# A kernel's first stage: small loads first, tokens and modulation weights in turn, tensor work in the order of landing, dummy products in the waits

## The chip, the cores and the metric

One core of a Trainium2 chip. The metric is the time of one execution on the device in microseconds; the median over several runs counts. A profiled execution gives the rows shown here.

## The reference

One layer of a hybrid backbone on 128 context tokens and 512 latent tokens of width 1024, all in float32. Each half has its own conditioning vector (`c_ctx` or `c`):

```python
mod = jax.nn.silu(cond) @ w_mod + b_mod
shift, scale, gate = jnp.split(mod, 3, axis=-1)
h = _rms(x, norm_pre_w) * (1 + scale[:, None, :]) + shift[:, None, :]
u = h @ w_in          # z, xbc, dt, q, k, v, g
...
out = mix @ w_out
y = x + gate[:, None, :] * _rms(out, norm_post_w)
```

Between `u` and `mix` stand a Mamba-2 scan (16 heads) and a retention scan (8 heads), both in two directions, in chunks of 128 tokens. The outputs are `y` for both halves and the context's final scan states.

## The kernel before

The 640 tokens are five token tiles t of 128 (tile 0 is the context), the model width is eight row blocks k of 128. A float32 product is made of three products of a faster type: each operand is split in a rounded part (`hh`, `w0h`, `whi`) and the rest (`hl`, `w0l`, `wlo`), and high x high, high x low and low x high are summed in PSUM.

The kernel has three parts: the first stage, which is in question; then a long middle in which the columns of `w_in` stream through 116 weight pieces (`ws`) while the scans are run as small jobs between the products; then the output product. The first stage makes the modulated tokens `h` (split, transposed, `hh` and `hl`), which the whole middle reads, and beside it multiplies them with the first 512 columns of `w_in` into five PSUM banks (`acc`, one a token tile). When the last of these is done, the first products of the middle (`gt`) follow.

The order of the first stage is written out by hand in `START`, a text of operations that a loop near line 352 emits. A letter is an operation, the number behind it is k or t:

- `M` (`load_wm`, L247): loads modulation weights of block k, 1024 KB, on SP's queue; three buffers. `W` (`load_w0`, L252): loads the block of `w_in`, 256 KB; three buffers. `L` (`load_x`, L258): loads a token tile, 512 KB; five buffers. `C`: two tables of 520 and 256 KB that the middle needs.
- `N` (`norm_x`): the token tile's sum of squares on ACT (L274), its power -0.5 on POOL, and the scaling of its first 128 columns on DVE (L279). `R` (`rest_x`): scales the other 896.
- `A` (`mod_a`): 16 TensorE records that multiply silu of the conditioning with the modulation block (`mod<-wm,silc`), and a copy `ms` on DVE (L297). `B` (`mod_b`): four products that turn the result into columns (`mod<-idt,ms`), and two DVE operations that make shift and scale of the block (`ash`, L317 and L318).
- `S` (`split0`): `w0h` on ACT (L306) and `w0l` on DVE.
- `H` (`h_tile`): for block k and the listed token tiles, transposes on TensorE (`tr`, L325), shift and scale on ACT (L329), and the split into `hh` (L332) and `hl` on DVE. It needs `B` of the block and `N` (or `R`) of the tokens.
- `G` (`gemm0`): three products `acc` of 512 columns for each listed token tile. It needs `H` and `S`.
- `Z` (`warm`): four dummy products of 128 x 128 zeros (`warm<-wz`) for each unit of its number; nothing reads them.
- `F` (`feed`): loads the first pieces of the middle's weights.

The transposes, `A` with `B`, and `Z` share three PSUM banks (`pi`); `A`'s bank is held until both `ash` are made. Each engine works its instructions in order. The order of the text is a preference: the framework that builds the kernel plans each engine's queue from it, and can put an instruction whose operands come earlier ahead of one that stands before it. The packed constants `pk` (108 KB: conditioning vectors, norms, biases) and `idt` (65 KB: the identity for the transposes) are loaded on ACT's queue at the start (lines 141 and 142).

Of the kernel before, what the change touches and what calls it, by code (L numbers as in the profile page):

```python
# [25 lines left out]
Z0, XS0, B0, C0, DT0, Q0, K0, V0, G0 = 0, 1024, 2048, 2560, 3072, 3104, 3616, 4128, 5152  # L26
# [15 lines left out]


START = """
M0 Z2 W0 L0 L1 L2 L3 L4 M1 W1 M2 N0 S0 A0 B0 H0:0 G0:0 R0 Z4 N1 H0:1 N2 N3 R1 H0:2 G0:1 H0:3 W2 M3
N4 W4 R2 R3 H0:4 R4 A1 S2 G0:4 W3 G0:3 B1 S1 S3 G0:2 H1:4 A2 W5 H1:0123 M4 B2 M5 H2:012 H2:3 H2:4
G1:01 G1:2 G2:12 G2:3 A3 G1:34 G2:4 B3 H3:0123 S4 G2:0 A4 H3:4 M6 G3:012 B4 H4:0123 H4:4 A5 G3:34 C0
M7 W7 S5 W6 B5 H5:0123 G4:012 A6 G4:34 F2 S6 B6 H5:4 H6:0123 H6:4 G5:012 A7 G5:34 F2 B7 S7 H7:0123
G6:34 G6:012 H7:4 F2 G7:012 G7:34
"""  # L50


# [53 lines left out]
def body(ctx, tc, io):  # L106
    nc = tc.nc
    vec, act, pool, sp, pe = nc.vector, nc.scalar, nc.gpsimd, nc.sync, nc.tensor
# [28 lines left out]
    pk = const.tile([P, PK_N], F32, name="pk")  # L137
    cst = const.tile([P, CN], F32, name="cst")
    idt = const.tile([P, P + 2], F32, name="idt")
    rope = const.tile([P, 4, 2, 64], F32, name="rope")  # L140
    act.dma_start(out=pk, in_=io["pk"])
    act.dma_start(out=idt, in_=io["idt"])
    tl = const.tile([P, 1], F32, name="tl")
    vec.memset(tl, 0.0)
    act.activation(tl, tl, AF.Tanh)
# [1006 lines left out]
```

## Time and profile before

| | |
|---|---|
| median of 3 runs | 608.21 us (607.2 to 610.53) |
| profiled execution | 606.02 us, its span 604.0 us, mean granted clock 0.993 |
| TensorE, VectorE, ScalarE, GpSimd busy | 582.3, 418.1, 337.4, 31.3 us |
| moved by DMA | 87.44 MB, 145 GB/s on average |
| first product of the middle | at 62.74 us of the span |

A slice of the page is 15.1 us long, so the first stage is the first four of 40. PE is TensorE's products, PEld its weight loads, DVE is VectorE, ACT is ScalarE, POOL is GpSimd, SP issues nearly all loads. A name such as `acc<-w0h,hh` is the written tile and the read ones. An engine that is 96% busy by this count need not be at its peak, since matrix products are pipelined and their ends are modelled.

### The profile page before, as it was taken

The page shows a single profiled execution, that of the slowest core. Times are in us where ns is not written, and L with a number is a line of the kernel's source. Part 1 is how long each engine was busy: PE and PEld are TensorE (multiplying, and loading weights), DVE is VectorE, ACT ScalarE, POOL GpSimd, SP SyncE. Part 2 cuts the span into 40 slices and gives each one's busy share as a digit, 9 for nine tenths or more (in the row PEclk, how much of TensorE's full clock was granted, in tenths as well). Part 3 has the DMA queues.
Part 4 walks back from the last instruction along what each step waited for, and adds up shares of the span by engine and source line. Part 5 has one row for each costly group of instructions (what it writes and reads, how often), then busy time and mean ns, then how long its engine had stood idle before and what let it go on. Part 6 is the DMA issues. An engine that isn't in the chain of part 4 may idle for free.

```text
span 604.0 us, 10966 instructions
## 1 busy us (share of the span) xinstructions
PE 582.3 (96%) x3833; PEld 521.5 (86%) x3833; DVE 418.1 (69%) x942; ACT 337.4 (56%) x934; POOL 31.3 (5%) x112
## 2 busy tenths in 40 slices
PE   5899998999999999999999999999999999999995
PEld 3577998978999998889999888999999777788895
DVE  3657498855698866668897746798867866743665
ACT  5436255665667764465766646566755857262421
POOL 1000001200000010000011000000110000000010
PEclk9899999999999999999999999999999999999998
DMA  8694231553335633232554223354537777384033
GB/s 348 229 362 161 63 105 48 162 146 109 99 97 159 185 91 86 80 122 70 189 172 112 76 69 105 102 163 131 160 96 223 209 266 221 116 272 120 18 109 135
DMA packets 47638, 87.44 MB, mean 145 GB/s; under 512 B 5792, under 2 KB 18656, under 8 KB 46048
## 3 DMA queue, kind: packets, MB, share of 16 engines
q1 hardware_dynamic: 47296, 86.57, 45.2%
q8 instruction: 30, 0.49, 0.3%
q14 instruction: 24, 0.20, 0.1%
q10 hardware_dynamic: 288, 0.18, 0.1%
HBM read 75.03 MB, written 9.60 MB: 140 GB/s over the span
## 4 chain that ended last, share of the span: by engine, by line
PE 65%; DVE 13%; ACT 9%; DMA 6%; issue 5%; POOL 2%; SPq 0%; POOLq 0%; DVEq 0%; ACTq 0%
PE gw L123 24%; PE gc L123 11%; PE gt L123 9%; PE acc L123 5%; PE go L123 4%; DMA cf<-cumd 3%; PE ss L123 2%; PE mod L123 2%; DVE wlo L131 2%; DVE SC L128 2%; PE sfb L123 1%; PE ry L123 1%; POOL sm L131 1%; DVE yc L128 1%; ACT jk L733 1%
## 5 line engine op out<-in xcount | busy, mean ns | idle before, releaser
L131 DVE TENSOR_TENSOR wlo<-raw,whi 128x512 fp32r<-128x512 f32 (+1 forms) x120 | 82.2, 690 | 49.2 <-ACT whi L174 48.3
L174 ACT CAST whi<-raw 128x512 fp32r<-128x512 f32 (+1 forms) x120 | 73.6, 619 | 76.3 <-PE gw L123 46.1
L123 PE MATMUL gc<-hh,whi 128*128 128x320 f32 x384 | 96.7, 331 | 0.0
L123 PE MATMUL gc<-hl,whi 128*128 128x320 f32 x384 | 88.3, 310 | 0.0
L123 PE MATMUL gc<-hh,wlo 128*128 128x320 f32 x384 | 87.6, 309 | 0.0
L123 PEld LDWEIGHTS gc<-hh,whi 128*128 128x128 f32 x384 | 63.9, 189 | 1.1
L123 PEld LDWEIGHTS gc<-hl,whi 128*128 128x128 f32 x384 | 64.3, 188 | 0.1
L123 PEld LDWEIGHTS gc<-hh,wlo 128*128 128x128 f32 x384 | 64.1, 188 | 0.0
L123 PE MATMUL gw<-whi,hh 128*128 128x512 f32 x120 | 50.6, 421 | 0.8 <-ACT u L484 0.8
L123 PE MATMUL gw<-whi,hl 128*128 128x512 f32 x120 | 47.0, 392 | 0.0
L123 PE MATMUL gw<-wlo,hh 128*128 128x512 f32 x120 | 46.8, 390 | 0.0
L123 PE MATMUL gt<-whi,hh 128*128 128x256 f32 (+1 forms) x160 | 46.3, 289 | 0.0
L123 PE MATMUL gt<-wlo,hh 128*128 128x256 f32 (+1 forms) x160 | 45.7, 286 | 0.0
L123 PE MATMUL gt<-whi,hl 128*128 128x256 f32 (+1 forms) x160 | 45.7, 286 | 0.0
L862 ACT ACTIVATE m<-gu,dt 128x128 f32<-128x128 f32 x80 | 31.3, 391 | 16.5 <-DVE gu L131 14.6
L834 ACT ACTIVATE cf<-cf,dmc 128x128 f32<-128x128 f32 x80 | 26.5, 393 | 18.4 <-DMA cf<-cumd 18.4
L131 DVE TENSOR_TENSOR m<-m,cf 128x512 f32<-128x512 f32 x40 | 27.5, 689 | 8.8 <-ACT cf L863 8.2
L123 PE MATMUL gw<-whi,mrh 128*128 128x512 f32 x80 | 32.3, 404 | 0.0
L123 PE MATMUL gw<-wlo,mrh 128*128 128x512 f32 x80 | 31.2, 391 | 0.0
L123 PEld LDWEIGHTS gt<-whi,hh 128*128 128x128 f32 x160 | 30.5, 190 | 0.7 <-issue 0.5
L863 ACT ACTIVATE cf<-gu,dt 128x128 f32<-128x128 f32 x80 | 31.0, 387 | 0.0
L123 PE MATMUL gw<-whi,mrl 128*128 128x512 f32 x80 | 30.9, 391 | 0.0
(232 smaller groups left out, 1327.8 us busy)
## 6 DMA issues: line engine op xcount, KB each, us to landing
raw<-ws SPq DMA_DIRECT2D x116, 256.0 KB, 2.8
cf<-cumd SPq DMA_DIRECT2D x20, 512.0 KB, 4.2
wm<-wm SPq DMA_DIRECT2D x8, 1024.0 KB, 8.2
mraw<-mixd SPq DMA_DIRECT2D x16, 320.0 KB, 3.4
ef<-ecumd SPq DMA_DIRECT2D x32, 128.0 KB, 3.3
wg<-wg SPq DMA_DIRECT2D x4, 1024.0 KB, 5.9
x<-x SPq DMA_DIRECT2D x5, 512.0 KB, 7.3
mixd<-rmix SPq DMA_DIRECT2D x20, 128.0 KB, 2.7
```

The lines of the kernel that those rows point to most:

```text
L123: r = pe.matmul(out, lhsT=a, rhs=b, start=start, stop=stop)
L128: eng.scalar_tensor_tensor(out=out, in0=in0, scalar=s, in1=in1, op0=op0, op1=op1)
L131: return eng.tensor_tensor(out=out, in0=a, in1=b, op=op)
L174: act.copy(hi, raw)
L733: act.activation(jk, yc[:, h], AF.Square, scale=P ** -0.5, accum_out=sm[:, 2 + h:3 + h])
L834: act.activation(cf[:, e, 1, q], cf[:, e, 1, q], AF.Identity, bias=dmc[:, c, h:h + 1])
L862: act.activation(m[:, e, q], gu[:, 0], AF.Copy, scale=dt[:, c, h:h + 1])
L863: act.activation(cf[:, e, 1, q], gu[:, 1], AF.Copy, scale=dt[:, c, 16 + h:17 + h])
```

## The change

`pk` and `idt` go to SP's queue, ahead of all other loads. The order of the first stage is rewritten:

- Loads: before, M0, W0, all five tokens, M1, W1, M2. After: L0, M0, W0, L1, L2, M1, W1, L3, L4, M2.
- Dummies: before, Z2 at the start and Z4 behind the first token's products (24 products). After: Z14 at the start, then Z1, Z4, Z3 and Z2 (96 products).
- Work: block 1 for tokens 0 to 2 (`H1:012`, `G1:012`) comes ahead of tokens 3 and 4. From block 3 on, `B` and `H` of the next block stand behind both halves of `G`, where they stood between the halves or further ahead.
- The second stage's first pieces (first `F2`) are loaded ahead of W6, M7 and W7, where they stood behind them.

```diff
-M0 Z2 W0 L0 L1 L2 L3 L4 M1 W1 M2 N0 S0 A0 B0 H0:0 G0:0 R0 Z4 N1 H0:1 N2 N3 R1 H0:2 G0:1 H0:3 W2 M3
-N4 W4 R2 R3 H0:4 R4 A1 S2 G0:4 W3 G0:3 B1 S1 S3 G0:2 H1:4 A2 W5 H1:0123 M4 B2 M5 H2:012 H2:3 H2:4
-G1:01 G1:2 G2:12 G2:3 A3 G1:34 G2:4 B3 H3:0123 S4 G2:0 A4 H3:4 M6 G3:012 B4 H4:0123 H4:4 A5 G3:34 C0
-M7 W7 S5 W6 B5 H5:0123 G4:012 A6 G4:34 F2 S6 B6 H5:4 H6:0123 H6:4 G5:012 A7 G5:34 F2 B7 S7 H7:0123
-G6:34 G6:012 H7:4 F2 G7:012 G7:34
+L0 M0 W0 L1 L2 M1 W1 L3 L4 M2 Z14 N0 S0 A0 Z1 B0 H0:0 Z4 N1 G0:0 R0 H0:1 Z3 N2 R1 G0:1 H0:2 A1 S1 R2 G0:2 B1
+H1:012 N3 W2 Z2 G1:012 H0:3 M3 N4 G0:3 R3 A2 H0:4 H1:3 G0:4 R4 G1:3 B2 H1:4 S2 G1:4 H2:0123 H2:4 W3 M4
+G2:012 A3 G2:34 B3 S3 H3:0123 W4 H3:4 M5 G3:012 A4 G3:34 B4 S4 H4:0123 H4:4 W5 C0 M6 G4:012 A5 G4:34 F2
+B5 S5 H5:0123 H5:4 W6 M7 G5:012 A6 G5:34 F2 B6 S6 H6:0123 H6:4 W7 G6:012 A7 G6:34 F2 B7 S7 H7:0123 H7:4
+G7:012 G7:34
...
-    act.dma_start(out=pk, in_=io["pk"])
-    act.dma_start(out=idt, in_=io["idt"])
+    sp.dma_start(out=pk, in_=io["pk"])
+    sp.dma_start(out=idt, in_=io["idt"])
```

## The prediction

> **What bounds the kernel now.** I read the page first, then the chain of waits in order of time for the first 80 us, then the windows and the timeline of the same stretch.
>
> ```profile
> span 604.0 us, 10966 instructions
> ...
> PE   5899998999999999999999999999999999999995
> ```
>
> TensorE is the bound, except in the first two of 40 slices (15.1 us each). Whatever the change can win lies there; behind it time is only shifted. The span of 604.0 belongs to an execution of 606.0 us, 2.2 under the median of 608.2; I predict a difference and put it on the median.
>
> ```profile
> 6.88 1.98 PE mod L123 x16
> ...
> 20.13 1.87 PE mod L123 x16
> ...
> 35.10 0.34 PE mod L123 x4
> ...
> 52.21 1.00 PE mod L123 x16
> 53.21 1.60 PE acc L123 x6
> 54.81 0.34 PE mod L123 x4
> 55.15 0.50 PE tr L325 x4
> 55.65 3.49 PE acc L123 x15
> 59.14 0.11 PE tr L325
> 59.24 3.49 PE acc L123 x15
> 62.74 15.99 PE gt L123 x120
> ```
>
> Columns: start, duration, who. The first stage ends at 62.74, where the second one's products (gt) begin. Warm prices: the 15 products of one row block k (G) 3.49, its 16 modulation products (A) 1.00, its 4 selecting products (B) 0.34, a transpose 0.11 to 0.13. One block is 3.49 + 1.00 + 0.34 + 5 x 0.12 = 5.4, eight are 43.5 us. So 19 us of the stage are no work. The page hides one cause:
>
> ```profile
> 10.00:12.00 2.00, 1.31 (x10) 1.16 (x11) 0.89 (x4) 1.04 (x4) 0.54 (x1) 1.00 1.02 420
> ...
> 16.00:18.00 2.00, 0.55 (x3) 0.26 (x2) 1.49 (x6) 0.84 (x3) 0.83 (x1) 1.00 0.97 404
> 18.00:20.00 2.00, 1.14 (x3) 0.45 (x2) 1.80 (x5) 0.46 (x1) 0.00 (x0) 0.76 1.10 439
> 20.00:22.00 2.00, 2.00 (x18) 0.67 (x17) 0.00 (x0) 0.00 (x0) 0.00 (x0) 0.50 0.86 346
> ```
>
> Columns: stretch, then busy time of PE, PEld, DVE, ACT, POOL, then granted clock, DMA share, GB/s. PE waits from 16 to 19 for the last token tiles, and then real work runs at clock 0.50: the same 16 modulation products cost 1.87 at 20.13 and 1.00 at 52.21. All loads together run at 404 to 439 GB/s until 22.
>
> **The change, part by part.** *Loads.* These rows are the issue of the third modulation block M2, its landing, and the loads issued between 1 and 2 us (size, us from issue to landing):
>
> ```profile
> 7.44 0.43 SPq L247 DMA_DIRECT2D wm<-wm  x1
> ```
> ```profile
> wm<-wm SPq DMA_DIRECT2D x1, 1024.0 KB, 11.4
> ```
> ```profile
> x<-x SPq DMA_DIRECT2D x1, 512.0 KB, 6.5
> raw<-w SPq DMA_DIRECT2D x1, 256.0 KB, 5.7
> pk<-pk ACTq DMA_DIRECT2D x1, 108.0 KB, 5.4
> idt<-idt ACTq DMA_DIRECT2D x1, 65.0 KB, 5.9
> ```
>
> M2 lands at 7.44 + 11.4 = 18.84. Before M2 the two orders load the same set (pk, idt, M0, M1, W0, W1, five tokens), so M2 lands there again, and the others lie ahead of it by their sizes at 420 GB/s, 410 KB per us: L4 16.3, L3 15.1, W1 13.8, M1 13.2, L2 10.7, L1 9.5, W0 8.2, M0 7.6. The gain is M1. Its place in the old order is behind all tokens: M1 then lands one M2 and one W1 ahead of 18.84, 15.7, and PE reached it at 20.13. The loss is that the first modulation products start near 7.6 and not 6.88.
>
> *The move of pk and idt.* On ACT's queue their issues took 0.41 and 0.46; on SP's they stand ahead of all loads:
>
> ```profile
> 0.72 0.41 ACTq L141 DMA_DIRECT2D pk<-pk  x1
> 1.16 0.46 ACTq L142 DMA_DIRECT2D idt<-idt  x1
> ```
> ```profile
> SPq L258 <- DMA pk<-pk: 2.3, 1, 2.3
> ```
>
> The first token's issue starts 0.9 later than M0's did, at 1.6. The engines stay idle until about 2 anyway, so every landing slips by 0 to 0.9; I take 0.3, since 173 small KB are under way meanwhile. pk, which landed at 0.72 + 5.4 = 6.1 and held the first products, lands near 3 and is off the path; should it stay late, M0 at 7.6 covers it. ACT is freed 0.9 earlier, which nobody waits for. The last row shows SP's ninth load waiting for the landing of the first one (pk). In the new order these partners (L0 ahead of L4, M0 ahead of M2) land long before the engines run dry: 0. In a sentence of its own: the Trainium skill, "DMA: Bandwidth & Descriptors", section "Issuing engines are not separate DMA queues", says that loads issued by different engines share the same 16 engines and that a second issuer saves issue time only. The trace agrees (pk, 108 KB, took 5.4 us from its own queue beside M0); by that rule alone the move costs its 0.9 of issue and the result would be 0.6 above mine.
>
> *Dummy products.*
>
> ```profile
> 11.33 1.91 PE L123 MATMUL warm<-wz 128*128 128x128 bf16 x16
> ```
>
> Cold, they start every 0.107 us: Z14 is 56, ends at 1.0 + 6.0 = 7.0 at the latest and delays nothing that lands at 7.6. Z1, Z4, Z3, Z2 (40 products, at most 4.3 cold, half of that warm) stand in the waits for tokens 1, 2 and M1; PE is in order, so one that comes late holds real products for at most 1.9: I take 0, range 0 to 1.
>
> In sentences of their own: the Trainium skill, "TensorE: Matmul & The Clock Gate", part 1, says that the array runs at half rate by default, at full rate after a busy window of 3.4 us, and falls back after an idle one. The trace agrees in the fall (clock 0.50 after the wait of 16 to 19); by the rule PE would be at full rate from 7 on.
>
> *PE's work up to B3.* With M1 at 13.2 + 0.3, A1 ends at 14.5. What follows is priced by this chain for the fourth block:
>
> ```profile
> 35.70 0.22 DVE L317 TENSOR_SCALAR ash<-mod,pk 128x2 f32<-128x2 f32 x1
> 35.83 0.27 DVE L318 TENSOR_SCALAR ash<-mod,bs,pk 128x2 f32<-128x2 f32 x1
> 36.22 1.02 ACT L329 ACTIVATE h<-tr,ash 128x128 f32<-128x128 f32 x2 [1.16 <-DVE ash L318]
> 37.27 0.43 DVE L332 CAST hh<-h 128x512 fp32r<-128x512 f32 x1 [1.17 <-ACT h L329]
> ...
> 37.55 0.66 PE L325 MATMUL tr<-idt,x 128*128 128x128 f32 x4
> 37.69 0.42 DVE L297 COPY ms<-mod 128x256 f32<-128x256 f32 x1
> ```
>
> ms 0.42 and B1 0.34 end near 15.4; from the end of B (35.44 = 35.10 + 0.34) to the end of hh (37.70) it is 2.26. So G1 for tokens 0 to 2 starts at 17.7. Done by then: A0, A1, B0, B1, nine products (2.1), six transposes: 5.5 us of work. Up to the end of B3 the list has 3 x 3.49 + 4 x 1.34 + 16 x 0.12 = 17.8. The other 12.3 put B3's end at 30.0 if PE is never idle. DVE is close to full then (1.80 of 2 us at 18 to 20 with the token work alone, and here the split, two ash, hh and hl of block 1 join it), so I add 0.5: 30.5, against 35.44. Lead 4.9. Of this, 1.5 is the cold stretch that goes (0.24 x 2 + 0.50 x 2 from the clocks of 18 to 22).
>
> *From B3 to the end.* Before: 62.74 - 35.44 = 27.3, PE without gaps, because B of the next block stands between the two halves of G. The new list puts B after the whole of G and H straight behind B. So the 2.26 from B to hh lies open; PE has A of the next block (1.00) and transposes (0.6) to put in it. If B always comes there, a block costs 2.26 + 3.49 + 0.34 = 6.1; if the engine order lets the next B slip into the wait as well, the block after it is ready at once, and that one costs 5.5. The builder does pull ready work ahead: four transposes at 37.55 belong partly to the next block's H, which the list puts behind the products that follow them. The next B is ready only after A and ms, 0.7 + 1.07 + 0.42 = 2.2 behind B, just when hh is: half and half, 5.8 a block. The last part is 2.26 + 3.49 = 5.75, four blocks are 23.2, together 29.0 (27.8 to 30.2): 1.7 of the lead is given back.
>
> *The sum.* 4.9 - 1.7 = 3.2 earlier: stage end 59.5 for 62.74, profiled run 602.8, median 605.0. The second stage is covered: its first weights are issued ahead of W6 now. Should their splits still end near 60, they would hold a few products by under 1 us.
>
> **Rivals.** *Slower: A isn't pulled ahead.* The list has A in the middle of G. If a PSUM bank (three for all of these) keeps it there, 2.26 a block holds transposes alone, and a block costs 2.26 + 3.49 + 1.00 + 0.34 = 7.1: 5.75 + 4 x 7.1 = 34.1, 6.8 more than before, less the lead of 4.9: 1.9 slower, 610.1. It decides from (27.3 + 4.9 - 5.75) / 4 = 6.6 a block. For it: the next A needs the bank that B's block frees only with the second ash, at 36.10. Against: 36.10 is 0.66 behind B, early enough.
>
> *The dummies don't keep the clock up.* The windows say 1.00 from 10 to 12, yet the dummies there run at 0.107 apiece, cold, so partly filled stretches may not raise the clock. Then real work meets one more stretch like that of 18 to 22, 1.5 more: 606.5.
>
> *The chain is hidden.* If B slips in every time and DVE holds nothing up: B3 at 30.0, 27.8 to the end: 57.8, 4.9 earlier, 603.3; with 0.9 less of early waits 602.4.
>
> **How the numbers follow.** Forecast 0.5 (603.6 to 606.2), hidden chain 0.2, cold clock or late DVE 0.18, A not pulled 0.12. A measurement of this kernel tells about 0.5%, 3.0 us, from no change. Under 605.2 lie the hidden chain and somewhat over half of the forecast: faster 0.49. Over 611.2 lies a third of the slower rival: 0.04. The rest, 0.47, is the same. The range runs from 602.0 (hidden chain) to 609.0 (into the slower rival).
>
> **What would show it.** Right: pk landed near 3, A1 near 13.5, clock 1.00 and modulation products at 1.0 from 8 on, B3 near 30.5, blocks of 5.5 and 6.1 in turn, gt first at 59.5. Wrong: products of acc at twice their time after 17; A in the middle of G with PE idle 2 us behind each B; B3 later than 32; gt early but the span unchanged, which would mean that a later stage gave it back.

## The result and the profile after

The changed kernel is slower: 611.19 us against 608.12, ratio 1.0057 (95% interval 1.0040 to 1.0073). The forecast was 605.0, range 602 to 609, so the time lies above the range. A second timing of the same kernel gave 610.98 and 1.0058 (1.0035 to 1.0080). Two of the 20 executions behind the 611.19 took 1480 and 2030 us; the ratio leaves them out, and the median of the other 18 is 611.00.

First a mistake of mine in the sections above. `Z14` does not stand for 56 products. The loop that emits the text reads one digit (`k = int(op[1])`, L353), so `Z14` is `Z1`: four products. The change has 44 dummies, not 96, and a wait of six microseconds at the start that I had filled is empty. The page of the changed kernel says so in its totals (before: x3833 on PE, so 20 more and not 72):

```profile
PE 584.4 (96%) x3853; PEld 523.8 (86%) x3853; DVE 417.4 (69%) x942; ACT 337.1 (55%) x934; POOL 31.5 (5%) x112
...
PE   4999998989999999999999999999999999999995
```

The first slice fell from 5 to 4 tenths. The view of the tile of the dummies (count, shortest, median and longest duration in ns, first and last start) shows the number, and in the median of 314 the cold clock:

```profile
L123 PE MATMUL warm<-wz x44: 217/314/331, 1.0 to 20.8; 128*128 128x128 bf16 x44
```

The chain of waits of the kernel after, in the columns used above:

```profile
8.40 1.93 PE mod L123 x16
...
18.37 1.00 PE mod L123 x16
...
22.48 3.06 PE acc L123 x12
...
36.69 0.34 PE mod L123 x4
...
43.80 1.07 PE mod L123 x16
...
55.31 0.34 PE mod L123 x4
...
57.84 0.58 PE mod L123 x4
...
58.69 7.01 PE acc L123 x30
65.70 14.39 PE gt L123 x108
```

The first 16 modulation products take 1.93 at 8.40, half clock, and those of block 1 start only at 18.37. B3 ends at 37.03 (36.69 + 0.34; before 35.44), and the stage ends at 65.70 (before 62.74). These 2.96 us agree with the 3.1 by which the medians differ. The second timing's profile has the stage end at 65.65 and a time of 608.85, 2.8 above the profile of before; the one shown here (610.78) lost more later on, which I leave aside.

The dummies also cost something while they run cold. The timeline of the kernel after (start, duration, engine and line; in brackets idle time and what ended it):

```profile
14.78 0.22 DVE L332 CAST hh<-h 128x128 fp32r<-128x128 f32 x1
...
15.23 1.29 PE L123 MATMUL warm<-wz 128*128 128x128 bf16 x10
...
16.32 0.42 PE L325 MATMUL tr<-idt,x 128*128 128x128 f32 x1
...
16.78 0.46 ACT L329 ACTIVATE h<-tr,ash 128x128 f32<-128x128 f32 x1 [2.45 <-PE tr L325]
```

`hh` of token 1 is done at 15.00 and its products could follow the last `acc` at once. Ten dummies stand ahead of them and of the next transpose until 16.32, and ACT waits 2.45 us for that transpose.

### The profile page after: what moved, and what is told of

Same layout as the page of the kernel before. It is cut to its first block, busy times and chain, and to the rows that moved or that the text cites. A ratio compares the mean times of both kernels' runs of the same rounds, so it can differ in the third digit from the quotient of the medians.

```text
span 608.9 us, 11002 instructions
## 1 busy us (share of the span) xinstructions
PE 584.4 (96%) x3853; PEld 523.8 (86%) x3853; DVE 417.4 (69%) x942; ACT 337.1 (55%) x934; POOL 31.5 (5%) x112
## 4 chain that ended last, share of the span: by engine, by line
PE 69%; DVE 11%; ACT 7%; DMA 6%; issue 5%; POOL 2%; SPq 0%; POOLq 0%; DVEq 0%; ACTq 0%
PE gw L123 24%; PE gc L123 13%; PE gt L123 9%; PE acc L123 5%; PE go L123 4%; DMA cf<-cumd 4%; PE mod L123 2%; PE ss L123 2%; PE sfb L123 2%; DVE SC L128 1%; DVE wlo L131 1%; POOL sm L131 1%; PE ry L123 1%; PE sy L123 1%; DVE yc L128 1%
## 5 line engine op out<-in xcount | busy, mean ns | idle before, releaser
L837 ACT ACTIVATE cf<-cf,ncf 128x128 f32<-128x128 f32 x80 | 26.4, 394 | 9.0 <-DVE cf L131 9.0
L123 PEld LDWEIGHTS gt<-whi,hh 128*128 128x128 f32 x160 | 30.5, 191 | 0.7 <-issue 0.5
```

The costliest lines, as they stand in the source:

```text
L123: r = pe.matmul(out, lhsT=a, rhs=b, start=start, stop=stop)
L837: act.activation(cf[:, e, 0, q], cf[:, e, 0, q], AF.Exp, bias=ncf[:, c, h:h + 1])
```

## The experiments

They were timed in three lists, each against its own runs of the kernel before (medians 607.43, 608.06 and 607.52): e1 to e4, e5 to e8, e9 to e12. Between lists only ratios are compared. "After" and "before" name the kernel that each one edits; the stage end is the start of the first `gt` in its profile. Each run has one profile, of a single execution. Stage ends and medians go the same way in most runs, but their differences from the kernel before lie up to 2.6 us apart, so a stage end alone settles nothing finer than that.

**e1: the dummies that the text meant.** After, with

```diff
-... L4 M2 Z14 N0 S0 A0 ...
+... L4 M2 Z7 Z7 N0 S0 A0 ...
```

> The changed kernel with the first dummies written as Z7 Z7 (56 products in place of the 4 that Z14 gives, since the loop reads one digit). Theory 1, the missing 52 dummies leave TensorE cold until 17.7 and that is most of the loss: modulation products of block 0 take 1.0 instead of 1.93, clock full from 8 on, A1 near 15.5 instead of 18.3, first product of the middle near 62.5 instead of 65.7, time 3 us under the changed kernel, about 608. Rival 2, the dummies in the waits hold real work: no better than the changed kernel by more than 1 us. Rival 3, the later landings or the late order cost it: within 1 us of the changed kernel, 611.

606.05, ratio 0.9984 (0.9969 to 0.9999), stage end 63.38. Its dummies and its chain:

```profile
L123 PE MATMUL warm<-wz x96: 216/220/314, 1.0 to 18.4; 128*128 128x128 bf16 x96
```
```profile
10.19 0.84 ACT hl L274
...
12.80 0.95 POOL rs L131
...
15.31 0.74 PE acc L123 x2
16.04 1.00 PE mod L123 x16
...
20.15 3.07 PE acc L123 x12
...
24.63 0.68 DVE w0l L131
...
25.51 1.66 PE acc L123 x6
...
34.36 0.34 PE mod L123 x4
...
63.38 11.73 PE gt L123 x88
```

The median dummy is 220 ns, not 314, and block 1 is 2.3 us earlier (16.04 for 18.37). All of that is still there at the stage end (63.38 for 65.70). The missing 52 products are 0.73% (0.9984 against 1.0057), more than the whole loss of the change. That is 4.4 us, about twice what the stage end shows. Yet the gain that I forecast from 96 is not there either: the stage still ends 0.64 later than in the kernel before.

**e2: no dummies in the waits.** After, without `Z1`, `Z4`, `Z3` and `Z2`; the four at the start stay.

> The changed kernel without the dummies Z1, Z4, Z3 and Z2 in the waits; the 4 at the start stay. Rival 2 (in-order dummies hold real work, 1.1 us in front of token 1's products and 1.5 in front of token 2's transpose): A1 near 16.5, stage end near 63.5, time near 609. Theory 1 (the clock is what counts): TensorE stays cold beyond 20, the stage ends at 66 or later, time 611 to 613.

608.37, ratio 1.0021 (0.9999 to 1.0042), 0.36% better than the kernel after, though the two intervals just overlap. The profile shows a gain and a loss:

```profile
17.23 1.39 PE mod L123 x16
...
21.69 4.47 PE acc L123 x12
```

Without the 40 dummies A1 starts 1.1 us earlier (17.23 for 18.37) and G1 0.8 (21.69 for 22.48); so much the cold dummies hold back. But the twelve products of G1 then take 4.47 us instead of 3.06, at half clock (0.51 from 21.50 to 24.90), and the stage ends at 66.31, 0.6 later than in the kernel after. So this profile does not show where the 0.36% come from. It is one of the slower executions of this kernel (609.39); whether the others kept their clock there is open.

**e9: dummies at the start alone.** e1 without `Z1`, `Z4`, `Z3`, `Z2`.

> Full dummies at the start, none in the waits (Z1, Z4, Z3, Z2 left out). If the 56 at the start are enough because real work then fills the windows: same as with all dummies, 606 (0.998). If the clock falls in the waits for tokens 1 and 2 (6.5 to 16): one half-speed window back, products of acc at 0.43 apiece for a while, stage end 1 to 2 us later, 607.5.

609.14, ratio 1.0018 (0.9998 to 1.0037): 0.34% worse than e1. So the 40 products in the waits are needed once the start is warm. The other way round, without them the 52 at the start are worth nothing: e9 and e2 differ only in those, and have ratios of 1.0018 and 1.0021 and stage ends of 66.56 and 66.31. The windows of e9, cut where the granted clock changes (the columns as above):

```profile
4.60:8.00 3.40, 1.41 (x25) 1.24 (x22) 0.29 (x1) 1.15 (x2) 0.54 (x1) 1.00 0.99 403
8.00:11.40 3.40, 2.98 (x20) 1.50 (x21) 1.02 (x2) 1.77 (x3) 0.01 (x1) 0.50 1.05 436
18.30:21.70 3.40, 2.05 (x21) 1.25 (x13) 1.82 (x6) 1.14 (x3) 0.00 (x0) 1.00 1.00 400
21.70:25.10 3.40, 3.18 (x8) 2.54 (x9) 1.93 (x6) 1.67 (x4) 0.81 (x1) 0.50 1.02 414
```

PE was busy 1.41 and 2.05 of 3.40 us, and each time the next 3.4 us ran at clock 0.50, at 8.0 just as A0 began. This first fall can't be put down to the edit: up to A0 TensorE has the same products in e1 (`Z1` stands behind A0), and e1 kept its clock. What differs is when the clock had risen: the pace of the dummies doubles near 4.6 in e9 and near 5.8 in e1. What sets the two kernels apart comes later, and over twelve executions each: the mean clock is 0.986 to 0.996 in e9 and 0.995 to 0.998 in e1.

**e3: the late part with the next block ahead.** After, with `B` and `H` of the next block between the halves of `G` again, and `A` one block further ahead:

```diff
-... G3:012 A4 G3:34 B4 S4 H4:0123 H4:4 W5 C0 M6 G4:012 A5 G4:34 F2 B5 S5 H5:0123 ...
+... A4 G2:34 G3:012 B4 S4 H4:0123 H4:4 W5 C0 M6 A5 G3:34 G4:012 B5 S5 H5:0123 ...
```

> The changed kernel with B and H of the next block put back between the halves of G, and A a block further ahead, from block 3 on. My step in question, the open chain behind B: blocks of 5.6 instead of 6.2, from B3's end to the end of the stage 27.3 instead of 28.7, time 1.4 to 2 us under the changed kernel, 609.5. If the chain isn't what makes a block 6.2, no difference: 611.

608.50, ratio 1.0010 (0.9990 to 1.0030), 0.47% better than the kernel after, stage end 63.81; blocks cost 5.65 on average instead of 6.2. But from B3's end to the end of the stage it is 28.5 us (35.32 to 63.81) and not 27.3: this order leaves six products of block 2 (`G2:34`) behind B3, and in front of its last block the chain behind B lies open. Of the 1.9 by which the stage ends earlier, 1.7 are there at B3 already (35.32 for 37.03).

**e5: e1 and e3 together.**

> Both edits at once: the 52 missing dummies at the start and the late order with B and H between the halves of G. If the two losses are separate, the gains add: modulation products 1.0 from the first on, blocks of 5.6 behind B3, stage end near 61.8, time 604.3 (0.994 to 0.995 of the kernel before). Rival: the last block's chain or the second stage's splits eat the second gain: no better than the full dummies alone, 606.

605.87, ratio 0.9958 (0.9940 to 0.9977), stage end 61.41 (e1: 63.38). The gain over e1, 0.26%, is less than the two intervals are wide. Its last block:

```profile
55.18 0.35 PE mod L122 x4
...
55.96 1.20 DVE wlo L130 x2
57.16 0.43 DVE hh L331
```

Two weight splits of the middle (1.20 us) stand ahead of the last `hh` on DVE, but they hold it up by next to nothing: ACT writes `h` in the same time (56.10 to 57.47), and `hh` ends 2.06 us behind the end of B7 (55.53 to 57.59). In e8, where no split stands there, the same step takes 2.04 (60.70 to 62.74, see its rows). What holds the last block up is the open chain from B to `hh` itself.

**e4 and e6: the queue of `pk` and `idt`.** e4 is before with the two loads on SP; e6 is e1 with them back on ACT.

> The kernel before with pk and idt on SP's queue alone, in front of M0. If each landing slips by the 0.9 us that their issues take and the stage follows the last tokens: 0.5 to 1 us over the kernel before, 609. If the earlier pk (near 3 instead of 6.1) or other slack covers it: no difference, 608.

> Full dummies, and pk and idt back on ACT's queue, so that L0 and M0 are issued 0.9 earlier. If the early stage follows the landings: M0 near 7.4 instead of 8.3, all of the stage 0.5 to 0.9 earlier, 605.3. If the chain over ACT and DVE for the tokens is what ends last: within 0.3 of the full dummies, 606.0. If pk lands behind L0 and M0 at 7 or later, A0 waits for it and nothing is won.

e4 607.53, ratio 1.0004 (0.9985 to 1.0024); e6 606.06, ratio 0.9987 (0.9968 to 1.0006) against 0.9984 for e1. The move is worth nothing that can be measured in the time, in either order. The profiles do show it: with the two loads on SP the stage ends 0.27 earlier in the old order (62.47 for 62.74) and 0.65 later in the new one (63.38 for 62.73).

**e8: the old order of loads under the new order of work.** e1 with `M0 W0 L0 L1 L2 L3 L4 M1 W1 M2`.

> Full dummies, the changed work order, but the loads in the old order (M0, W0, five tokens, M1, W1, M2). If loading tokens and modulation in turn is worth its 1.8 us earlier M1: A1 at 17 or later instead of 16.0, stage end 1 us later, 607. If A1 waits for the tokens' chain anyway (it ran 2.1 after M1's landing): the same, 606, or a little better since the tokens come 1.2 earlier.

611.57, ratio 1.0065 (1.0042 to 1.0089). The chain:

```profile
5.49 11.69 DMA wm<-wm
...
17.31 1.07 PE mod L123 x16
...
21.43 3.06 PE acc L123 x12
...
60.35 0.35 PE mod L123 x4
...
62.30 0.44 DVE hh L332
...
62.79 3.77 PE acc L123 x15
```

Block 1 now waits for M1, and G1 starts 1.3 later than in e1 (21.43 for 20.15). The rest of the 3.2 at the stage end (66.55 for 63.38) arises at the last block, where the engine order no longer has B7 slip into the wait (60.35). Under the new order of work, then, the loads in turn are worth 0.8%; by the profile more than half of that came through the change of the engine order.

**e7 and e11: the old order with dummies.** e7 is before with more dummies at the start; e11 adds nine units in the waits for tokens 2 to 4 and changes nothing else:

```diff
-M0 Z2 W0 L0 L1 ... R1 H0:2 G0:1 H0:3 W2 M3
+M0 Z7 Z7 W0 L0 L1 ... R1 H0:2 G0:1 Z4 H0:3 Z5 W2 M3
```

> The kernel before with 56 dummies at the start in place of its 8; nothing else. If a cold TensorE in the first 22 us costs the kernel before anything: modulation products of block 0 1.0 instead of 1.98, stage end 1 to 2.5 us earlier, 605.5 to 606.5. If the wait for the last token tiles (16 to 19 us, by loads, ACT and POOL) sets the pace and cools the clock again: within 0.5 of the kernel before, 607.4.

> The kernel before with 56 dummies at the start (as in the run before this) and 16 and 20 more in its waits between 13 and 18 us (Z4 behind token 1's products, Z5 behind the transpose for token 3); nothing else. If the clock is what the waits cost: no fall to 0.50 at 18.4, the modulation products of block 1 at 1.0 instead of 1.86, 1 to 1.5 us under the same kernel with the start dummies alone, 604.8. If the dummies come late and hold the transposes for tokens 3 and 4: no gain, 606.1.

e7 606.10, ratio 0.9969 (0.9941 to 0.9997); e11 602.83, ratio 0.9925 (0.9899 to 0.9952), which beats both kernels. The two intervals overlap a little; e11's stage also ends 1.2 earlier (60.36 for 61.56). The windows of e7 and of e11 over the wait in which the kernel before lost its clock, for e11 with the two ahead of it:

```profile
15.00:18.40 3.40, 1.22 (x5) 0.44 (x3) 2.90 (x9) 1.22 (x4) 0.72 (x1) 1.00 1.02 411
18.40:21.80 3.40, 3.40 (x21) 1.80 (x21) 0.67 (x2) 0.00 (x0) 0.00 (x0) 0.50 1.03 413
```
```profile
7.90:11.30 3.40, 1.62 (x23) 1.55 (x21) 1.83 (x6) 2.97 (x6) 1.08 (x2) 1.00 1.03 419
11.30:14.70 3.40, 3.32 (x13) 2.06 (x10) 2.83 (x10) 3.11 (x7) 1.46 (x2) 0.50 1.03 423
14.70:18.10 3.40, 2.59 (x39) 2.16 (x37) 2.65 (x9) 1.56 (x4) 0.72 (x1) 1.00 1.02 406
18.10:21.50 3.40, 3.40 (x28) 2.23 (x29) 1.45 (x5) 0.00 (x0) 0.00 (x0) 1.00 1.01 408
```

And e11's chain there:

```profile
18.84 1.00 PE mod L123 x16
...
60.36 5.72 PE gt L123 x43
```

The wait is as long, but dummies fill it (PE 2.59 instead of 1.22), the clock stays at 1.00, and the modulation products after it take 1.00 instead of 1.87 (before). Even so e11 has not held its clock throughout: it was at 0.50 from 11.30 to 14.70, after an earlier wait. The stage ends 2.4 earlier than before (60.36 for 62.74).

**e10: everything of the new order that paid.** e5 with the two small loads on ACT and block 7's `B` and `H` ahead of all of `G6`:

```diff
-... A7 G5:34 G6:012 B7 S7 H7:0123 H7:4 F2 G6:34 G7:012 G7:34
+... A7 G5:34 B7 S7 H7:0123 G6:012 G6:34 H7:4 F2 G7:012 G7:34
```

> Full dummies, the late order, pk and idt on ACT's queue, and B7 with H7 ahead of all of G6, as the kernel before had it. In the run with both edits the last block's hh waited 1.2 us behind two splits of the second stage and a chain of 2.3. If that is all that is left: from B7 to the end of the stage 7.9 with no gap, stage end near 59.6, time 603.5 to 604.5 (0.993). Rival: the gain is off the path, as with the queue alone: 605.9.

603.30, ratio 0.9932 (0.9907 to 0.9957). The chain's end:

```profile
53.49 3.49 PE acc L122 x15
57.09 3.49 PE acc L122 x15
```

The last two blocks run without a wait between them, and the stage ends at 60.58. With dummies at the start and in the waits, the new order repaired (e10) and the old order untouched (e11) are equal within their intervals.

**e12: the kernel after again**, beside e9 to e11; its numbers stand with the result.

> The changed kernel once more beside the others. By theory 1 TensorE is cold until 17 to 18.5 whatever the phase of the clock's windows, stage end 65.5 to 66.5, 3 us over the kernel before: 1.005. If the first measurement had caught an unlucky phase: 1.002 or less and a stage end under 64.5.

## Why the prediction was wrong, point by point

*What bounds the kernel: right in the main.* What the stage gains or loses reaches the end, to within the 2.6 us named above, and the clock lost in the wait of 16 to 19 was worth having: e7 to e11, in which only dummies are added in the waits, is 0.44%, about 2.7 us.

*Loads: nearly right.* pk landed near 3, as forecast, but M1 and M2 slipped by more. (One row was misread beside it: the loads run at 404 to 439 GB/s until 20; from 20 to 22 it is 346.) SP's row for M2, and the landing rows of M1 and M2 in the kernel after:

```profile
8.29 0.33 SPq L247 DMA_DIRECT2D wm<-wm  x1
```
```profile
wm<-wm SPq DMA_DIRECT2D x1, 1024.0 KB, 9.5
...
wm<-wm SPq DMA_DIRECT2D x1, 1024.0 KB, 11.4
```

M2 landed at 8.29 + 11.4 = 19.7, 0.85 behind before; I had taken 0.3 of a possible 0.9. By the rule that I had cited beside it (the Trainium skill, "DMA: Bandwidth & Descriptors", "Issuing engines are not separate DMA queues") the whole issue time is lost. The runs don't decide between the two: the move alone makes M1 and M2 land 0.4 later in the old order (e4: 16.05 and 19.2 for 15.7 and 18.84), and 0.7 and 0.4 later in the new one (e1: 13.8 and 20.5; e6: 13.1 and 20.1), but with the same loads M2 lands at 19.7 in the kernel after and at 20.5 in e1. M1, issued at 4.39, landed at 13.9 for my 13.5. None of this moved the time (e4, e6).

*Dummies: the step that failed.* "Z14 is 56" was wrong, and with it "PE at full rate from 7 on": A0 took 1.93 at 8.40, and products at full rate start only near 17.7. The 52 products are worth 0.73% (e1). The price "0, range 0 to 1" for dummies that hold real products was at its upper bound on the cold clock: 1.1 at A1 and 0.8 at G1 (e2). My rival "The dummies don't keep the clock up" names the symptom, at 1.5 us, but not this cause, and its sum still counted the early block 1.

*PE's work up to B3: failed a second time, by itself.* I forecast A1's end at 14.5, G1 from 17.7, B3's end at 30.5. In e1, where all 96 dummies run, they are 17.04, 20.15 and 34.70; in the kernel after 19.37, 22.48 and 37.03. So the miss of 6.5 at B3 is 2.3 of missing dummies and 4.2 that remain in e1. Of these, 2.5 arise ahead of A1's end: M1 is there at about 13.9, but in TensorE's queue A1 stands behind two `acc` products of token 2, whose tiles come through ACT, POOL and DVE (10.19, 12.80, 15.31 in e1's chain). I had priced A1 by its load alone. From A1's end to G1 my 3.2 holds (3.1). From G1 to B3 I had 12.8, the sum of the work and 0.5 for DVE; it is 14.55 in both kernels. Hardly any of that is waiting: in e1 TensorE is busy for 14.24 of it, as far as the modelled ends of its products tell. The same work cost more than the warm prices, since it ran in short pieces:

```profile
27.82 0.62 PE mod L123 x2
...
29.34 0.57 PE mod L123 x8
29.91 2.29 PE acc L123 x9
32.20 0.56 PE mod L123 x6
```

A3, cut in runs of 2, 8 and 6, took 1.75 instead of 1.00. The 36 products of `acc`, in runs of 12, 6, 3, 9 and 6, took 9.5 instead of the 8.4 that 3.49 for 15 would make. DVE's work is in the chain only from 24.27 to 25.51 (`w0l` at 24.63); with B2 and two transposes in that gap, about 0.6 of work, it cost some 0.7, not far from the 0.5 that I had put. So the term that I had mis-sized is the work itself, priced by long runs; why short ones cost more is not shown. That A1 would run earlier if it stood ahead of token 2 is read from the chain and was not tried.

*From B3 to the end: right in the sum by luck, wrong inside.* 28.67 for my 29.0. But blocks did not cost 5.5 and 6.1 in turn: three cost 6.2 (36.69 to 55.31), then the last B slipped into the wait (57.84, 2.5 behind the one before), and both last blocks ran as one row of 30 products. Three blocks 0.4 dearer than the 5.8 I took and a last part of 7.3 for 5.75 were made up for by one block of 2.8. A stands in the wait each time (43.80), so the slower rival, A not pulled ahead, is false although the time came out on its side. That the late order costs time is shown by e3 (0.47%) and agrees with e5 (0.26%). The 1.4 by which 28.67 exceeds the 27.3 of before is not its size: before has three products of block 2 behind its B3 (`G2:0`) and after has none, and e3 and e5 gain ahead of B3, with 28.5 behind it.

*The sum.* The 52 missing dummies cost 0.73%, as long as the 40 in the waits are there, and the late order 0.3 to 0.5%; the queue costs nothing that the time shows. With both put right the new kernel is 0.4% (e5) to 0.7% (e10) faster than before. But the old order with dummies alone is 0.75% faster (e11). So no run shows that the early order of work and the loads in turn earn anything beside the dummies; e8 shows only that in this order of work the loads are needed.

## What to carry to other kernels

Count a text's operations in the trace or by the parser, not by the eye: one row of the profile, the count of a tile, tells it. Where an engine waits on loads, holding its clock up may be worth as much as reordering the loads, and can be tried alone with a one-line edit; put dummies where the wait is certain, since on an engine that works in order, cold ones delay what stands behind them. Fill the later waits too: in the new order dummies at the start alone won nothing (e9 against e2). Price a step that is moved earlier by every chain that stands ahead of it in its engine's queue, not by its own load, and products that will run in short pieces by pieces of that length.

## What the runs showed of the hardware

The clock fell not only after empty stretches. In windows of 3.4 us it fell after PE had been busy for 1.22 (e7), 1.41 and 2.05 us (e9), and stayed after 2.59 (e11). The share alone does not decide: it fell in e11 after a stretch with 1.62 (longest gap 1.23), and in e1 it stayed at 1.00 after one with 1.63 (longest gap 1.77). To come back it took more: in e9 stretches with 2.98 and 2.48 left it at 0.50, and it rose after one with 3.34 (14.80 to 18.20).

```profile
5.70:9.10 3.40, 1.63 (x30) 1.15 (x28) 0.29 (x1) 1.28 (x3) 0.54 (x1) 1.00 1.01 410
9.10:12.50 3.40, 2.24 (x34) 1.79 (x27) 1.91 (x7) 2.67 (x5) 0.54 (x1) 1.00 1.03 431
```

What the clock counts stays open. The Trainium skill, "TensorE: Matmul & The Clock Gate", part 1, lets the rate fall after an idle window; here a stretch that was 60% busy was enough. A second point: the clock column says 1.00 for the first microseconds of every kernel, while the dummies there take 314 ns, as cold ones do, and 220 later (e1); in the kernel after it says so up to A1, though A0 took 1.93; early on, the duration of a known product tells the clock and the column does not.
